# Later stores, gate temporaries in operand slots, one table load per output product, and an end in two halves, in a two-layer hybrid block on one core

## The chip, the core and the metric

The kernel runs on one core of a Trainium2 chip. The core has five engines with instruction queues of their own: TensorE (PE, matrix products), VectorE (DVE), ScalarE (ACT), GpSimd (POOL) and SyncE (SP, which here only issues transfers). Sixteen DMA engines move data between the device's memory and the core. ACT, SP and POOL can each issue transfers; in the profile they have the queues q10 (ACT), q1 (SP) and q0 (POOL). The metric is device time in microseconds (us) of one execution.

## The reference

One sequence of 512 tokens of width 2048 goes through two layers in float32. Both have the same frame:

```python
xn = rms_norm(h, norm_pre[i])
...                                  # the layer's mixing, ending in a product with w_out
h = h + rms_norm(y, norm_post[i])
h = h + (p[i] @ ple_w_proj[i]) * jax.nn.sigmoid(h @ ple_w_gate[i])
```

Layer 0 mixes with 16 heads of an attention with forgetting ("fox") and 16 heads of a recurrent time mix ("rwkv"), both gated by silu; layer 1 is a gated MLP with a spatial mix over chunks of 128 tokens:

```python
u, v, g = _split(xn @ c_w_in[j], (GMLP_W, GMLP_W, GMLP_W))        # 2048 columns each
v = layer_norm(gelu(v), c_ln_g, c_ln_b)
mixed = einsum('gts,bnsgc->bntgc', w_s * causal, v in chunks of 128 tokens and 16 groups) + b_s
y = (gelu(u) * mixed * silu(g)) @ c_w_out[j]
```

## The kernel before

**The order of the program.** Layer 0's input products and its rwkv part run first (to 730 us), then fox with the last gates (730 to 1011), the output product (1011 to 1180), the product with `ple_w_proj` (to 1202) and the gate product with `ple_w_gate` (to 1380). Layer 1's input product follows (1380 to 1853) in parts named V, U0, G0, U1 and G1, of which V is twice as long as the others, then its output product (to 2023), the small product (to 2045), the gate product (to 2207) and the last store. All float32 matmuls are made of three passes of a narrower type: each operand is split into a high and a low part, `whi`, `wlo` for weights, `xh`, `xl` for the other side, and hi*hi, hi*lo and lo*hi are summed.

**The Strassen products.** The large products use Strassen's scheme: seven products of half the size, numbered 1 to 7, in place of eight. `seven` runs over them, and in each over eight *pieces* of weights, two casts and 12 (or 24 half as wide) matmuls apiece. `pieces` yields them: a weight tile `rq`, `raw` or `half`, loaded by SP or POOL, is cast on ACT (L1559, `whi`) and its rest taken on DVE (L1561, `wlo`). The sums of activations that Strassen needs are made on DVE by `sums` (L1428, L1429), cast on ACT (L974) and taken again on DVE (L975).

**What sets the order.** A scheduler places the instructions of each engine by priority and by data dependencies; each engine then runs its own list in order. Two devices steer it. `later(n, step)` puts a piece of side work into the program n piece rows after the present one, and `tick` hands it out. `row()` (L977) ties an instruction to the latest weight cast, `self.cast`: it is not issued before that. Side work without such a tie can be placed much earlier than its row.

**The places the change touches.**

- *The mixed u.* In `layer_c`, `mix` norms one group of v (L1690), mixes it (L1720 to L1722, matmuls from `sg`, the cast of L1713), and multiplies u in place (L1724). Each mix takes its v from the device's memory (`sq<-vd`, L1673) and three small tables (L1680, L1684), all issued on ACT's queue. The mixed u, two tiles `u[0]` and `u[1]` of four rows, goes back to memory by `saved` (L1765 to L1767): eight stores `yd<-xh`, also on ACT's queue. U1's gelu (L1657) writes over them later.
- *The last gates.* In `layer_ab`, `load` and `gate` (L2020 to L2030) multiply the outputs of fox and rwkv by silu of 16 gate blocks. Gates 7, 0, 1, 2 are the last. Their inputs (`gz`, and `vT` for those copied from PSUM at L2049) and tanh results (`th`) lie in the pool `fw`, in fox's memory. The output product's weight tiles `rq` reuse that memory. `yh` slots are the places of later operands.
- *The table.* `row_scale` (L1218) makes 1/rms from sums of squares. It calls `row_rstd`, which takes a logarithm and an exponential on ACT. With `self.last` given, the load of their function table is issued after that instruction (`ln_exp`, ACT_TABLE_LOAD at L370).
- *The gate's sums.* `first_gate` puts sums for layer 1's first Strassen products into the rows of the gate product: `s1`, `s24`, `x22`, `s3`, four of each. `s24(q)` without a second argument forms the sum of `s1(q)` again.
- *The end.* `last_layer`'s `emit` (L1365) takes a block of 128 x 512: sigmoid on ACT, a multiplication and an addition on DVE, a store by SP. `seven` calls it for product 3 (L1614) after a subtraction on DVE (L1615).

Of the kernel before, what the change touches and what calls it, by code (L numbers as in the profile page):

```python
# [16 lines left out]
P = 128  # L17
T = 512
# [88 lines left out]
class Net:  # L107
# [991 lines left out]
    def first_gate(self, H, state, wp, ps):  # L1099
# [85 lines left out]
        W = i["ple_w_gate"][0]  # L1185
        self.seven(FIRST(*[Pair(W, 2 * j * T, 2 * j, emit) for j in range(2)]), Sets(s), ps, fm=True)
        s1, s24, s3, x22 = C[3:]
        steps = [(8 + 2 * q, lambda q=q: s1(q)) for q in range(4)]
        steps += [(17 + 4 * q, lambda q=q: s24(q)) for q in range(4)]
        steps += [(35 + 3 * q, lambda q=q: x22(q, True)) for q in range(4)]  # L1190
        steps += [(48 + 3 * q, lambda q=q: s3(q)) for q in range(4)]
        return accq, last["act"], cs, steps
# [1 line left out]
    def out_product(self, layer, W, swap, s, steps, place, load_place, hd, src_place, op_place, wp, ps):  # L1194


        nc, tc, i = self.nc, self.tc, self.i
        npost = self.cols["norm_post"]
        H, Y = {}, {}
        accq = [self.t(wp, [P, T], "accq", bufs=1), self.rstdB]  # L1200
        seen = [False, False]

        def out_block(pr, m, n, src):
            e, q = m // 2, 2 * n + m % 2
            Y[q, e] = place(q, e).rearrange("p (a t) -> p a t", a=2)
            sv = src.rearrange("p (a t) -> p a t", a=2)
            for a in range(2):
                c = 16 * layer + 2 * q + a
                self.last = nc.scalar.activation(Y[q, e][:, a, :], sv[:, a, :], AF.Copy, scale=npost[:, c : c + 1])
            if seen[e]:  # L1210
                sq = self.t(wp, [P, T], "sq")
                nc.scalar.activation(sq, src, AF.Square)
                nc.vector.tensor_tensor(accq[e], accq[e], sq, ALU.add)
            else:
                nc.scalar.activation(accq[e], src, AF.Square)
            seen[e] = True

        def row_scale(e):  # L1218
            with tc.high_priority(HP):
                pt = self.t(ps, [P, 256], "mm")  # L1220
                for a in range(2):
                    nc.tensor.matmul(pt, self.ones, accq[e][:, a * 256 : a * 256 + 256], start=(a == 0), stop=(a == 1))
                self.row_rstd(pt, accq[e][:, :256], self.last)

        def load(q):
            for e in range(2):
                H[q, e] = load_place(q, e).rearrange("p (a t) -> p a t", a=2)
                nc.sync.dma_start(H[q, e], hd[:, 2 * q : 2 * q + 2, e * 256 : e * 256 + 256])

        def ple():  # L1230
            self.pops = [], []
            for j in range(2):
                src = src_place(j).rearrange("p (m c) -> p m c", c=P)
                nc.sync.dma_start(src, i["p"][layer, 0, :, j * P : (j + 1) * P].rearrange("(m p) c -> p m c", p=P))
                pt = self.t(ps, [P, T], "mm")
                for m in range(4):
                    nc.tensor.transpose(pt[:, m * P : (m + 1) * P], src[:, m, :], self.ident)
                for ops, n in zip(self.pops, (2 * j, 2 * j + 1)):
                    ops.append(op_place(n))
                self.finish(pt, self.pops[0][j], self.pops[1][j])  # L1240

        steps = steps + [(88 + 3 * q, lambda q=q: load(q)) for q in range(8)]
        steps += [(82, ple), (98, lambda: row_scale(0))]
        for n, step in sorted(steps, key=lambda x: x[0]):
            self.later(n, step)
        pairs = [Pair(W, 2 * j * T, 2 * j, out_block) for j in range(2)]
        for pr in pairs:
            pr.swap = swap
        self.seven(FIRST(*pairs), Sets(s), ps, fm=True)
        self.clock += 100  # L1250
        self.tick()
        rows = lambda e: accq[e][:, :256].unsqueeze(1).broadcast_to([P, 2, 256])
        return H, Y, row_scale, rows

    def last_layer(self, cp, fs, turn, wp, ps):
# [106 lines left out]
        for n, step in sorted(steps, key=lambda x: x[0]):  # L1362
            self.later(n, step)

        def emit(pr, m, n, src):  # L1365
            nc.scalar.activation(src, src, AF.Sigmoid)
            nc.vector.tensor_tensor(src, src, pj[n, m], ALU.mult)
            o = res[n, m]
            nc.vector.tensor_tensor(o, o, src, ALU.add)
            self.later(  # L1370
                2, lambda: nc.sync.dma_start(self.out[0, m * P : (m + 1) * P, n * T : (n + 1) * T], o)
            )

        W = i["ple_w_gate"][1]
        pairs = [Pair(W, 2 * j * T, 2 * j, emit) for j in range(2)]
# [190 lines left out]
    def seven(self, order, sets, ps, after=lambda n: None, fm=False):  # L1566
# [3 lines left out]
        for step, (pr, prod, keep) in enumerate(order):  # L1570
# [30 lines left out]
            for m in range(2):  # L1601
                a = acc[m]
                if prod in (1, 5):
                    if m == 0:
                        pr.R[prod] = self.t(self.rp, [P, 2, T], "comb")
                    with tc.high_priority(2 * HP):
                        nc.scalar.copy(pr.R[prod][:, m], a)
                elif prod == 2:
                    pr.emit(pr, m, pr.n, a)
                elif prod == 6:  # L1610
                    u2 = pr.R[1][:, m]
                    nc.vector.tensor_tensor(u2, a, u2, ALU.add)
                elif prod == 3:
                    with tc.high_priority(HP) if step == len(order) - 1 else nullcontext():  # L1614
                        nc.vector.scalar_tensor_tensor(a, a, -1.0, pr.R[1][:, m], ALU.mult, ALU.subtract)  # L1615
                        pr.emit(pr, m, pr.n + 1, a)
            pr.done.add(prod)
            if prod == 7:
                u3 = pr.R[7] = pr.R[1] if 3 in pr.done else self.t(self.rp, [P, 2, T], "comb")
# [12 lines left out]
    def layer_c(self, cp, sets, steps, accq, after, wp, ps):  # L1632
# [129 lines left out]
            for e in range(2):  # L1762
                self.later(at + e, lambda e=e: turn(q, e, lambda a, m: y[a][:, m, :]))

        def saved(n):  # L1765
            for m in range(4):
                nc.scalar.dma_start(self.yd2[:, 4 * n : 4 * n + 4, m, :], u[n][:, m, :].rearrange("p (g c) -> p g c", c=P))  # L1767

        def done(step):
# [30 lines left out]
                    for e in range(8):  # L1800
                        mix(8 * j + e, 42 + int(6.8 * e))
            if step == nv + 13:
                for n in range(2):
                    self.later(4, lambda n=n: saved(n))
            if step == nv + 21:
                for q in range(4):
                    early(q, 26 + 5 * q)
# [178 lines left out]
    def layer_ab(self, cp, pool):  # L1986
# [26 lines left out]
        with tc.tile_pool(name="fc", bufs=1) as fc, tc.tile_pool(name="fw", bufs=2) as fw:  # L2013
# [3 lines left out]

            gz = {}

            def load(n):  # L2020
                gz[n] = self.t(fw, [P, T], "gz")
                nc.sync.dma_start(gz[n], self.ahead[C_GATES[n]])

            def gate(n):

                z, th = gz.pop(n), self.t(fw, [P, T], "th")
                with tc.issue_after(self.fox_ready.ins):
                    nc.scalar.activation(th, z, AF.Tanh, scale=0.5)
                nc.vector.scalar_tensor_tensor(self.y[n], z, 0.5, self.y[n], ALU.mult, ALU.mult)
                nc.vector.scalar_tensor_tensor(self.y[n], th, 1.0, self.y[n], ALU.add, ALU.mult)  # L2030

            self.Y11 = self.place(("yh", 8))
# [11 lines left out]
            load(7)  # L2044
            for n in range(3):
                acc = dense(C_GATES[n])
                gz[n] = self.t(fw, [P, T], "vT")
                with tc.high_priority(2 * HP):
                    copies = nc.scalar.copy(gz[n][:, :256], acc[:, :256]), nc.vector.tensor_copy(gz[n][:, 256:], acc[:, 256:])  # L2049
                    self.entry = [x.ins for x in copies]  # L2050
                gate(n)
# [31 lines left out]
```

## Time and profile before

Three runs took 2209.56, 2212.39 and 2212.74 us. The profile is of a further execution.

| | us |
|---|---|
| median of three runs | 2212.39 |
| the profiled execution | 2215.19 |
| its span, first to last instruction | 2213.5 |
| PE busy, 16535 matmuls | 2184.2 (99%) |
| DVE busy | 1663.0 (75%) |
| ACT busy | 1356.6 (61%) |
| POOL busy | 299.7 (14%) |
| DMA queues q1, q0, q10: share of 16 engines | 35.0%, 22.5%, 2.2% |
| last matmul starts | 2207.1 |

PE's 99% do not say that it runs without a break: matmuls are pipelined and their ends modelled, so that each shown duration (0.39 us for 512 columns) is longer than the distance to the next (0.23 us). What PE loses is therefore read from its idle times, from the clock that it was granted, and from the chain of work that ended last. In all rows a line number is that of the kernel before. The words after `<-` in brackets are what ended the idle time before an instruction.

### The profile page before, as it was taken

How to read it: one execution, taken by the hardware profiler on the slowest of the kernel's cores; microseconds unless marked ns; L12 is line 12 of the kernel's file. 1: busy time of each engine (PE TensorE's matmuls, PEld its weight loads, DVE VectorE, ACT ScalarE, POOL GpSimd, SP SyncE). 2: the span in 40 equal slices, each digit the busy share in tenths (PEclk: the TensorE clock that was granted, in tenths of full speed). 3: DMA queues.
4: the chain of work that ended last, by engine and by line, in shares of the span. 5: the costliest groups of instructions: out<-in, count | busy, mean ns of one | idle time of the engine just before them, and what ended most of it. 6: DMA issues, size and time to landing. Idle time of an engine off the chain costs nothing.

```text
span 2213.5 us, 43467 instructions
## 1 busy us (share of the span) xinstructions
PE 2184.2 (99%) x16535; PEld 1875.3 (85%) x16535; DVE 1663.0 (75%) x3228; ACT 1356.6 (61%) x2764; POOL 299.7 (14%) x360
## 2 busy tenths in 40 slices
PE   8999999999999999999999999999999999999998
PEld 7878888888888788888998999788887889999887
DVE  8756677657633678886978988997686688978978
ACT  5545555555544577775767757766575577757754
POOL 2001010101000000000220121111220221120031
PEclk9999999999999999999999999999999999999999
DMA  7322322223233733336797889788778787688796
GB/s 237 95 79 58 89 78 77 74 64 92 68 87 99 220 102 94 103 88 181 150 205 256 213 190 237 178 217 223 179 168 215 174 197 189 148 197 267 206 244 170
DMA packets 304143, 343.34 MB, mean 155 GB/s; under 512 B 15757, under 2 KB 187950, under 8 KB 302910
## 3 DMA queue, kind: packets, MB, share of 16 engines
q1 hardware_dynamic: 237438, 240.93, 35.0%
q0 software_dynamic: 44608, 85.99, 22.5%
q10 hardware_dynamic: 21888, 13.64, 2.2%
q8 instruction: 130, 2.13, 0.4%
q14 instruction: 79, 0.65, 0.1%
HBM read 305.61 MB, written 34.90 MB: 154 GB/s over the span
## 4 chain that ended last, share of the span: by engine, by line
PE 83%; DVE 6%; DMA 4%; issue 4%; ACT 3%; SPq 0%; ACTq 0%; POOL 0%; DVEq 0%; POOLq 0%
PE mm L1596 43%; PE mm L213 9%; PE mm L215 9%; PE mm L214 9%; DVE wlo L1561 2%; PE tm L551 1%; DMA rq<-in_ple_w_gate_dram 1%; PE tm L572 1%; PE g L923 1%; DMA sq<-vd 1%; PE tm L484 1%; PE tm L910 1%; PE pp L340 1%; ACT whi L197 1%; PE ch L636 1%
## 5 line engine op out<-in xcount | busy, mean ns | idle before, releaser
L1559 ACT CAST whi<-rq 128x512 fp32r<-128x512 f32 x485 | 299.0, 620 | 211.7 <-PE mm L1596 133.4
L1561 DVE TENSOR_TENSOR wlo<-rq,whi 128x512 fp32r<-128x512 f32 x485 | 331.6, 690 | 111.7 <-ACT whi L1559 109.6
L213 PE MATMUL mm<-xh,whi 128*128 128x512 f32 x992 | 412.1, 415 | 0.0
L215 PE MATMUL mm<-xh,wlo 128*128 128x512 f32 x992 | 391.8, 395 | 0.0
L214 PE MATMUL mm<-xl,whi 128*128 128x512 f32 x992 | 389.8, 393 | 0.0
L197 ACT CAST whi<-raw 128x512 fp32r<-128x512 f32 x272 | 167.5, 617 | 151.0 <-PE mm L214 106.3
L199 DVE TENSOR_TENSOR wlo<-raw,whi 128x512 fp32r<-128x512 f32 x272 | 186.1, 696 | 94.1 <-ACT whi L197 71.3
L215 PEld LDWEIGHTS mm<-xh,wlo 128*128 128x128 f32 x992 | 186.4, 188 | 41.3
L213 PEld LDWEIGHTS mm<-xh,whi 128*128 128x128 f32 x992 | 187.0, 189 | 33.2
L214 PEld LDWEIGHTS mm<-xl,whi 128*128 128x128 f32 x992 | 187.3, 189 | 29.8
L1596 PE MATMUL mm<-whi,xl 128*128 128x512 f32 x424 | 137.9, 392 | 0.8 <-DVE xl L975 0.4
L1596 PE MATMUL mm<-whi,yh 128*128 128x512 f32 x424 | 137.6, 393 | 0.0
L1596 PE MATMUL mm<-whi,yl 128*128 128x512 f32 x420 | 137.6, 393 | 0.0
L1561 DVE TENSOR_TENSOR wlo<-raw,whi 128x512 fp32r<-128x512 f32 x154 | 105.3, 690 | 40.1 <-ACT whi L1559 39.5
L1559 ACT CAST whi<-raw 128x512 fp32r<-128x512 f32 x154 | 94.9, 620 | 65.8 <-PE mm L1596 50.9
L1596 PE MATMUL mm<-xh,whi 128*128 128x256 f32 x696 | 126.9, 283 | 0.0
L1596 PEld LDWEIGHTS mm<-xh,whi 128*128 128x128 f32 x696 | 108.7, 192 | 0.1
L1504 POOL DMA_DIRECT2D rq<-in_c_w_in_dram x56 | 68.3, 1220 | 244.4 <-DVE wlo L1561 154.1
L1596 PE MATMUL mm<-xh,wlo 128*128 128x256 f32 x348 | 98.5, 283 | 0.0
L1561 DVE TENSOR_TENSOR half<-rq,half 128x512 fp32r<-128x512 f32 x111 | 76.5, 689 | 26.9 <-ACT half L1559 26.6
L1596 PE MATMUL mm<-xl,whi 128*128 128x256 f32 x520 | 95.5, 284 | 0.1
L1596 PEld LDWEIGHTS mm<-whi,xl 128*128 128x128 f32 x424 | 79.6, 188 | 18.2 <-DVE xl L975 0.9
(531 smaller groups left out, 5168.3 us busy)
## 6 DMA issues: line engine op xcount, KB each, us to landing
raw<-in_ab_w_in_dram SPq DMA_DIRECT2D x128, 512.0 KB, 3.9
rq<-in_c_w_in_dram POOLq DMA_DIRECT2D x56, 512.0 KB, 6.7
rq<-in_c_w_in_dram SPq DMA_DIRECT2D x50, 512.0 KB, 4.9
rq<-in_ple_w_gate_dram SPq DMA_DIRECT2D x44, 512.0 KB, 5.9
rq<-in_ple_w_gate_dram POOLq DMA_DIRECT2D x36, 512.0 KB, 9.1
raw<-in_c_w_in_dram SPq DMA_DIRECT2D x26, 512.0 KB, 7.8
rq<-in_c_w_out_dram SPq DMA_DIRECT2D x24, 512.0 KB, 4.4
rq<-in_ab_w_out_dram POOLq DMA_DIRECT2D x20, 512.0 KB, 7.4
```

What stands on the lines that cost most here:

```text
L197: nc.scalar.copy(hi[:, : m * n], src)
L199: self.weng.tensor_tensor(lo[:, : m * n], src, f(hi[:, : m * n]), ALU.subtract)
L213: nc.tensor.matmul(acc, hi, xhi[k], start=(k == 0), stop=False)
L214: nc.tensor.matmul(acc, hi, xlo[k], start=False, stop=False)
L215: nc.tensor.matmul(acc, lo, xhi[k], start=False, stop=(k == nk - 1))
L340: nc.tensor.matmul(acc, mat, part, start=(j == 0), stop=(j == 1))
L484: nc.tensor.matmul(pg[q][:, e], BK[pp, e].rearrange("p a t -> p (a t)"), AR[pp, e, q::2, :], start=True, stop=True)
L551: nc.tensor.matmul(px[dst, e, :], a[src, e, :], b[src, e, :], start=True, stop=True)
L1504: nc.gpsimd.dma_start(view(tl), block(*where), accum_op=ALU.add)
L1559: self.cast = nc.scalar.copy(hi, src)
L1561: nc.vector.tensor_tensor(lo, src, f(hi), ALU.subtract)
L1596: nc.tensor.matmul(o, x, y, start=(first and r == 0 and j == 0 and not a), stop=(r == 7 and j == 2), **more)
```

## The change

Five edits:

1. `saved` is called once for each of the eight stores, at rows 7 to 14 after U1's start instead of twice at row 4, and each store is tied by `row()` to the cast of its row.
2. For gates 7, 0, 1 and 2, `gz` lies in the `yh` slots 4, 5, 6 and 7, and tanh is written in place, except for gate 2, whose tanh goes to `yh` slot 3. For gates 7, 0 and 1 the first multiplication comes before tanh.
3. `row_scale` loads no table; one load is placed at row 66 of each output product.
4. In `first_gate`, `s24(q, s1(q))` at rows 8, 13, 18 and 23 takes the place of `s1` at rows 8 to 14 and `s24` at rows 17 to 29.
5. In the last product's second block, subtraction, sigmoid, multiplication, addition and store are each done for 256 columns and then for the other 256.

```diff
         s1, s24, s3, x22 = C[3:]
-        steps = [(8 + 2 * q, lambda q=q: s1(q)) for q in range(4)]
-        steps += [(17 + 4 * q, lambda q=q: s24(q)) for q in range(4)]
+        steps = [(8 + 5 * q, lambda q=q: s24(q, s1(q))) for q in range(4)]
...
-                self.row_rstd(pt, accq[e][:, :256], self.last)
+                self.row_rstd(pt, accq[e][:, :256], None)
...
+        def table():
+            with self.row():
+                nc.scalar.preload_act_table_set(LNSET)
+
-        steps = steps + [(88 + 3 * q, lambda q=q: load(q)) for q in range(8)]
+        steps = steps + [(88 + 3 * q, lambda q=q: load(q)) for q in range(8)] + [(66, table)]
...
-        def emit(pr, m, n, src):
-            nc.scalar.activation(src, src, AF.Sigmoid)
-            nc.vector.tensor_tensor(src, src, pj[n, m], ALU.mult)
+        def emit(pr, m, n, src, parts=(slice(0, T),), ready=lambda x: None):
+            for x in parts:
+                ready(x)
+                nc.scalar.activation(src[:, x], src[:, x], AF.Sigmoid)
             o = res[n, m]
-            nc.vector.tensor_tensor(o, o, src, ALU.add)
-            self.later(
-                2, lambda: nc.sync.dma_start(self.out[0, m * P : (m + 1) * P, n * T : (n + 1) * T], o)
-            )
+            for x in parts:
+                nc.vector.tensor_tensor(src[:, x], src[:, x], pj[n, m][:, x], ALU.mult)
+                nc.vector.tensor_tensor(o[:, x], o[:, x], src[:, x], ALU.add)
+                to = self.out[0, m * P : (m + 1) * P, n * T + x.start : n * T + x.stop]
+                self.later(2, lambda x=x, to=to: nc.sync.dma_start(to, o[:, x]))
...
+                    def less(x, a=a, m=m):
+                        nc.vector.scalar_tensor_tensor(a[:, x], a[:, x], -1.0, pr.R[1][:, m, x], ALU.mult, ALU.subtract)
+
                     with tc.high_priority(HP) if step == len(order) - 1 else nullcontext():
-                        nc.vector.scalar_tensor_tensor(a, a, -1.0, pr.R[1][:, m], ALU.mult, ALU.subtract)
-                        pr.emit(pr, m, pr.n + 1, a)
+                        if step == len(order) - 1 and m:
+                            pr.emit(pr, m, pr.n + 1, a, (slice(0, T // 2), slice(T // 2, T)), less)
+                        else:
+                            less(slice(0, T))
+                            pr.emit(pr, m, pr.n + 1, a)
...
-        def saved(n):
-            for m in range(4):
+        def saved(n, m):
+            with self.row():
                 nc.scalar.dma_start(self.yd2[:, 4 * n : 4 * n + 4, m, :], u[n][:, m, :].rearrange("p (g c) -> p g c", c=P))
...
             if step == nv + 13:
-                for n in range(2):
-                    self.later(4, lambda n=n: saved(n))
+                for x in range(8):
+                    self.later(7 + x, lambda x=x: saved(x // 4, x % 4))
...
+            own = {7: 4, 0: 5, 1: 6, 2: 7}
+
             def load(n):
-                gz[n] = self.t(fw, [P, T], "gz")
+                gz[n] = self.slot("yh", own[n], F32) if n in own else self.t(fw, [P, T], "gz")
                 nc.sync.dma_start(gz[n], self.ahead[C_GATES[n]])
...
-                z, th = gz.pop(n), self.t(fw, [P, T], "th")
+                z = th = gz.pop(n)
+                if n == 2:
+                    th = self.slot("yh", 3, F32)
+                elif n not in own:
+                    th = self.t(fw, [P, T], "th")
+                if n in own and n != 2:
+                    nc.vector.scalar_tensor_tensor(self.y[n], z, 0.5, self.y[n], ALU.mult, ALU.mult)
                 with tc.issue_after(self.fox_ready.ins):
                     nc.scalar.activation(th, z, AF.Tanh, scale=0.5)
-                nc.vector.scalar_tensor_tensor(self.y[n], z, 0.5, self.y[n], ALU.mult, ALU.mult)
+                if n not in own or n == 2:
+                    nc.vector.scalar_tensor_tensor(self.y[n], z, 0.5, self.y[n], ALU.mult, ALU.mult)
...
-                gz[n] = self.t(fw, [P, T], "vT")
+                gz[n] = self.slot("yh", own[n], F32)
```

The order of instructions changes at three places of which the prediction speaks. In the order rows the lines are those of the kernel named; L1500 and L1559 of the kernel before are L1505 and L1564 of the changed one.

The first is ACT's list in G0's last rows, where the stores of the mixed u stand in the kernel before (L1767, `yd` from `xh`), among weight casts, a mix's tables (`accq`) and v (`sq`). Before:

```order
L1690 ACTIVATE sq_20053<-sq_20053,nb_17484,rv_17483 128x128 x3
L1767 DMA yd_36_104<-xh_3789_19158 128x4x128
L1559 CAST whi_20198<-rq_3993_20084 128x512
L1712 CAST w_4019_20208<-mm_20134 128x128
L1767 DMA yd_36_104<-xh_3789_19158 128x4x128
L1559 CAST whi_20218<-rq_3993_20084 128x512
L1680 DMA accq_20196<-in_c_ln_g_dram 128x128
```

The changed kernel, in U1's first product, up to its gelu (the table load of L1668 is L1657's before):

```order
L1778 DMA yd_36_104<-xh_3782_19146 128x4x128
L1778 DMA yd_36_104<-xh_3840_19415 128x4x128
L1564 CAST whi_20611<-rq_4098_20598 128x512
L1564 CAST whi_20624<-rq_4103_20622 128x512
L1778 DMA yd_36_104<-xh_3840_19415 128x4x128
L1564 CAST whi_20634<-rq_4103_20622 128x512
L1778 DMA yd_36_104<-xh_3840_19415 128x4x128
L1564 CAST half_4111_20650<-rq_4067_20457 128x512
L1778 DMA yd_36_104<-xh_3840_19415 128x4x128
L1564 CAST whi_20660<-rq_4067_20457 128x512
L1564 CAST whi_20671<-rq_4072_20479 128x512
L1564 CAST whi_20681<-rq_4072_20479 128x512
```

`xh_3782` is u[0], of which the fourth store is shown, and `xh_3840` is u[1]. No store stands in G0 any more; all eight stand between the casts of U1's first pieces, and the gelu's table load follows the last row.

The second is SP's list at the entry of the first output product, with the weight loads. Before:

```order
L1500 DMA raw_12752<-in_ab_w_out_dram 128x2x512
L1500 DMA raw_12792<-in_ab_w_out_dram 128x2x512
L1500 DMA raw_13070<-in_ab_w_out_dram 128x2x512
L1500 DMA raw_13104<-in_ab_w_out_dram 128x2x512
L1500 DMA rq_2602_12866<-in_ab_w_out_dram 128x2x512
L1500 DMA rq_2612_12911<-in_ab_w_out_dram 128x2x512
```

And in the changed kernel:

```order
L1505 DMA raw_12749<-in_ab_w_out_dram 128x2x512
L1505 DMA raw_12789<-in_ab_w_out_dram 128x2x512
L1505 DMA rq_2599_12863<-in_ab_w_out_dram 128x2x512
L1505 DMA rq_2609_12908<-in_ab_w_out_dram 128x2x512
L1505 DMA rq_2616_12948<-in_ab_w_out_dram 128x2x512
L1505 DMA rq_2621_12982<-in_ab_w_out_dram 128x2x512
L1505 DMA rq_2629_13023<-in_ab_w_out_dram 128x2x512
L1505 DMA raw_13067<-in_ab_w_out_dram 128x2x512
```

Five `rq` loads now stand ahead of two `raw` loads that they followed.

The third is ACT's list at the entry of the first gate product: scales and squares of the output blocks (L1209 and L1212 before, L1208 and L1211 changed), a weight cast, the table load, and the copies out of PSUM (L1093). Before:

```order
L1093 COPY yl_2976_15041<-mm_14991 128x512
L1209 ACTIVATE yh_2956_14968<-comb_14347,col_72_254 128x256
L197 CAST whi_15132<-raw_15114 128x512
L1209 ACTIVATE yh_2956_14968<-comb_14347,col_72_254 128x256
L1212 ACTIVATE sq_14971<-comb_14347 128x512
L1212 ACTIVATE sq_14978<-comb_12906 128x512
L1209 ACTIVATE yh_2960_14982<-comb_12906,col_72_254 128x256 x2
L197 CAST whi_15182<-raw_15180 128x512
L370 ACT_TABLE_LOAD
L1212 ACTIVATE sq_14985<-comb_12906 128x512
L1093 COPY yl_2977_15044<-mm_14992 128x512
```

And in the changed kernel:

```order
L1211 ACTIVATE sq_14975<-comb_12903 128x512
L1208 ACTIVATE yh_2957_14979<-comb_12903,col_72_254 128x256
L197 CAST whi_15178<-raw_15176 128x512
L1208 ACTIVATE yh_2957_14979<-comb_12903,col_72_254 128x256
L1211 ACTIVATE sq_14982<-comb_12903 128x512
L1093 COPY yl_2972_15035<-mm_14987 128x512
L1093 COPY yl_2973_15038<-mm_14988 128x512
L1093 COPY yl_2974_15041<-mm_14989 128x512
```

The table load is gone from here, and the first two copies, which stood ahead of the last squares, now come behind them.

## The prediction

> **What bounds the kernel now.** I read the page's chain first, then TensorE's (PE's) waits, then windows around the largest of them.
>
> ```profile
> PE 83%; DVE 6%; DMA 4%; issue 4%; ACT 3%; SPq 0%; ACTq 0%; POOL 0%; DVEq 0%; POOLq 0%
> ```
>
> PE is 83% of the chain that ends last, and the change takes away no matmul. So it can only win where PE stands still or runs slowly. PE's waits that lie near the edits (in all, times, longest):
>
> ```profile
> PE mm L1720 <- ACT sg L1713: 5.3, 1, 5.3
> PE mm L1596 <- ACT whi L1559: 2.4, 1, 2.4
> ...
> PE mm L999 <- ACT yl L1093: 0.9, 1, 0.9
> ...
> PE mm L1222 <- ACT yl L1093: 0.5, 1, 0.5
> PE mm L1596 <- DVE xl L975: 0.4, 1, 0.4
> PE mm L1596 <- ACT xl L974: 0.4, 1, 0.4
> ```
>
> Behind three of them stands a second loss, seen in windows (stretch, length, busy time of PE, PEld, DVE, ACT and POOL, then the clock granted to PE, DMA share, GB/s):
>
> ```profile
> 1025.00:1028.40 3.40, 3.40 (x18) 3.40 (x18) 3.20 (x7) 2.20 (x5) 1.43 (x2) 0.51 0.93 348
> 1195.60:1199.00 3.40, 3.30 (x8) 2.65 (x9) 0.40 (x2) 2.27 (x6) 0.00 (x0) 0.50 0.87 242
> 1675.20:1680.30 5.10, 5.10 (x12) 3.69 (x13) 3.89 (x6) 2.05 (x5) 0.00 (x0) 0.50 0.37 106
> ```
>
> Just after each stall PE's clock is 0.50 or 0.51. At half speed a stretch costs half its length: 1.7 us at 1025, 1.7 at 1195.6, 2.6 at 1675. The three places lose 2.4 + 1.7 = 4.1, 0.9 + 0.5 + 1.7 = 3.1 and 5.3 + 2.6 = 7.9 us: 15.1 in all. The change touches the cause of each.
>
> The Trainium skill ("TensorE: Matmul & The Clock Gate", Part 1: The HAM clock gate) says that the clock falls after at least one idle window of about 3.4 us. The rows differ: it fell after 2.4 us, and after 0.9 + 0.5. By the rule only the 7.9 us would go entirely and the two 1.7 us might stay, a gain lower by 3.4 us; I go by the rows.
>
> **Stores of the mixed u.** Why did PE wait 5.3 us? ACT's timeline has it:
>
> ```profile
> 1650.61 0.38 ACTq L1767 DMA_DIRECT2D yd<-xh  x1
> ...
> 1652.78 0.38 ACTq L1767 DMA_DIRECT2D yd<-xh  x1
> ...
> 1658.77 1.00 ACTq L1673 DMA_DIRECT2D sq<-vd  x1
> ...
> 1673.74 0.88 ACT L1690 ACTIVATE sq<-sq,nb,rv 128x128 f32<-128x128 f32 x2 [5.85 <-DMA sq<-vd]
> ```
>
> Two of the eight stores went out early and stand in ACT's DMA queue, q10, ahead of the next mix's three tables and of its v (sq<-vd). V arrived some 15 us after its issue. ACT stood 5.85 us on it, with the cast L1713 that PE wanted queued behind. What q10 moved (packets, MB, share) from 1650.6 to 1658.8, with the issues of a store and of a table in that stretch, and from 1658.8 to 1673.7:
>
> ```profile
> q10 hardware_dynamic: 762, 0.53, 27.8%
> ...
> yd<-xh ACTq DMA_DIRECT2D x2, 256.0 KB
> ...
> accq<-in_c_ln_g_dram ACTq DMA_DIRECT2D x1, 64.0 KB, 17.2
> ```
>
> ```profile
> q10 hardware_dynamic: 1080, 0.70, 16.3%
> ```
>
> It ran at 0.53/8.2 = 65 KB/us, then at 0.70/14.9 = 47. The sum, 1.23 MB, is two stores of 256 KB (0.52), three tables of 64 KB (0.20), this v (0.26 as a store), and 0.25 left over from before. Without the stores 0.71 MB remain, and by 1658.8 the left-over and the tables can be through (0.45 of the 0.53 moved by then). V's own 0.26 MB take 4.0 us at 65 and 5.6 at 47: it lands near 1663 to 1665, with 2 us on the way by 1667. ACT began its idle at 1673.74 less 5.85, at 1667.9. So v comes in time, or 0 to 0.8 us late. I take 7.9 us, the whole; bounds 4 and 8.3: under 4, v would land after 1670, at half the slower rate; the upper end adds the 0.4 that the store issues take ACT's queue.
>
> The stores move to rows 7 to 14 of U1's first product, eight within some 11 us. What is late next is U1's gelu, which overwrites the old u:
>
> ```profile
> 1714.84 1.28 ACT L1657 ACT_TABLE_LOAD   x1 [0.65 <-DMA yd<-xh]
> ```
>
> Today it waits 0.65 us, with four stores ahead of it in q10 from 1697.5 on. After the change four must land too, u[0]'s, since u[1]'s come behind; so about the same wait. A second wait is new: by the built program, the last two stores wait on ACT, ahead of its casts, for a landed u[0] store and for a weight load of this kind:
>
> ```profile
> 1701.70 3.74 SPq L1500 DMA_DIRECT2D raw<-in_c_w_in_dram  x2
> ```
>
> ```profile
> raw<-in_c_w_in_dram SPq DMA_DIRECT2D x2, 512.0 KB, 8.0
> ```
>
> Issued at 1701.7, it lands 8.0 us later, at 1709.7; the last store's place in ACT's order is that of the cast at 1709.5. More traffic may add some us: ACT waits 0 to 3. PE has casts in hand, as these rows show:
>
> ```profile
> 1665.91 0.63 ACT L1559 CAST half<-rq 128x512 fp32r<-128x512 f32 x1 [0.75 <-PE mm L1596]
> ```
>
> ```profile
> 1679.69 1.83 PE L1596 MATMUL mm<-half,yh 128*128 128x512 f32 x6
> ```
>
> Cast at 1665.9, read at 1679.7, less some 7.4 us lost in between: 6 us ahead, of which 2 are the cast and DVE's pass. Up to 4 us of ACT's wait is hidden: cost 0; beyond it PE pays one for one.
>
> **The entry of the output product.**
>
> ```profile
> 1002.70 0.58 ACT L928 COPY yl<-g 64x512 f32<-64x512 f32 x1 [0.53 <-PE g L923]
> ```
>
> ```profile
> 1014.83 0.70 DVE yl L2030
> 1015.62 6.79 DMA rq<-in_ab_w_out_dram
> ```
>
> ```profile
> 1022.48 1.14 ACT L1559 CAST whi<-rq 128x512 fp32r<-128x512 f32 x2 [3.09 <-DMA rq<-in_ab_w_out_dram]
> ```
>
> The first rq load lies in fox's memory, where the last gates' temporaries are alive until DVE's L2030 ends at 1015.5. In the change they lie in operand slots, and rq waits only for fox, whose last product is copied at 1002.70. SP then issues five rq loads from about 1003 to 1007, and at 6.8 us they land near 1010 to 1014, where the cast would take the first at 1019.4 (1022.48 less 3.09). The 2.4 us and the half clock behind them go: 4.1. The gates' instructions keep kind and number; where tanh is now in place it waits for DVE's first multiply, 0.69 us under PE's matmuls. But ACT and DVE are full here with the gates' casts, so up to 1 us of another wait may show, and with it the clock. I take 4; bounds 1 and 5.
>
> **Table loads.** In the entry of the gate product PE waits for ACT's copies out of PSUM:
>
> ```profile
> 1191.24 1.28 ACT L370 ACT_TABLE_LOAD   x1
> 1192.53 0.63 ACT L1212 ACTIVATE sq<-comb 128x512 f32<-128x512 f32 x1
> 1193.07 0.57 ACT L1093 COPY yl<-mm 128x512 f32<-128x512 f32 x1
> ```
>
> ```profile
> 1193.69 0.50 PE L999 MATMUL mm<-xl,whi 128*128 128x512 f32 x1 [0.94 <-ACT yl L1093]
> ```
>
> The load leaves: 1.28 us of ACT's queue ahead of those copies. But the new order also puts every block's scale and square ahead of the first copy, where two copies stood between them. Counting its rows by these durations, the first copy ends near 1192, and PE wants it about 0.9 us earlier: of 1.4 us of waits 0.9 remain, and the half clock perhaps not. I take 2 of the 3.1; bounds -0.5 (clock still down, the copy later yet) and 3.1. The one load that is left, at row 66, runs between casts for which ACT has time. The second layer has no such wait: 0.
>
> **The gate's sums.** Four sums leave DVE:
>
> ```profile
> L1428 DVE TENSOR_TENSOR sg<-yl,yl x16: 420/422/432, 1015.8 to 1080.2; 128x256 f32<-128x256 f32 x16
> L1428 DVE TENSOR_TENSOR sg<-yh,yh x16: 684/688/697, 1205.4 to 1432.2; 128x512 f32<-128x512 f32 x16
> ```
>
> That is 4 x 0.69 = 2.8 us of DVE work up to 1432, just ahead of layer C's first products, where PE waits 0.4 + 0.4 for xl. Earlier sums take both; other waits may take their place. 1 us, bounds -0.5 and 1.5.
>
> **The end in halves.** DVE, the serial tail, does six passes over 256 columns for three over 512. By the two rows above that is 6 x 0.42 - 3 x 0.69 = 0.45 more, less the overlap with ACT's sigmoid, and less half of the last store of 256 KB. 0, bounds -0.4 and 0.4.
>
> **The sum** is 7.9 + 4 + 2 + 1 + 0 = 14.9 us, from the profiled execution's 2215.2 to 2200.3. That execution lies 2.8 above the runs' median, 2212.4; part of that may be the stalls themselves. I take 13.4 from the median: **2199.0**.
>
> **The rivals.** *A: v still comes late.* q10 shares the DMA engines with POOL's and SP's loads, so v may land near 1670 without the stores too. PE then waits some 2.5 us plus a halved clock of 1.7: of the 7.9, 3.7 remain: 2199.0 + 4.2 = 2203, up to 2207. For it: v's margin of 1 us. Against it: the 0.52 MB counted above.
>
> *B, the slower side: the burst of stores holds ACT.* If the eight stores do not land in their order, u[0]'s last comes with the whole burst. 2.1 MB at the mean of 65 and 47 KB/us take 37 us, to 1734 on the old clock, where U1's gelu wants it at 1714.8. ACT's casts stand behind it; with 4 us hidden PE waits some 15 and runs 2.6 us of half clock: 2199.0 + 17.6 = 2217, and from 2211 if half of it. It decides from 4 us of ACT's idle at this table load. For it: nothing but the larger burst. Against it: today's 0.65 us behind four stores. The Trainium skill ("DMA: Bandwidth & Descriptors", Queues, rings and completion order) says that each engine takes a ring's descriptors in ring order, which speaks against it; no row here shows two stores of one queue apart.
>
> *C: the instructions move and the time does not.* Each stall removed uncovers the next one: four waits of other operands lie within 1 us behind the entry's, and weight loads, 3 to 8 us earlier for PE, are just in time. 2207 to 2212.
>
> **How the numbers follow.** Forecast (2193.5 to 2203) 0.58, A 0.18, B 0.10, C 0.14. No change means within 0.2%, 4.4 us, about what a measurement of this kernel can tell. Below 2208.0 lie the forecast, A and a third of C: faster 0.80. The rest of C and half of B are the same: 0.14. Slower 0.06. The range: 2193.5 is all terms at their upper bounds (8.3 + 5 + 3.1 + 1.5 + 0.4 = 18.3) off the median; 2208.5 takes in A and part of C and leaves under 0.2 out.
>
> **What would show it.** The wait of L1720 on L1713 is gone from PE's list, and no half clock stands where 1675 was; likewise at 1025 and 1195. The first rq load is issued near 1003. Two table loads are gone, and the one of row 66 has no wait of PE behind it. Wrong would be: ACT still idle for sq<-vd by over 2 us; ACT idle for over 4 us at a store or at U1's gelu; a PE wait on whi in U1.

## The result, and the profile after

The changed kernel takes 2200.21 us (median of five runs, 2198.46 to 2202.32) against 2212.39 (five runs): a ratio of 0.9949, 95% interval 0.9934 to 0.9963, or 11.3 us less (8.2 to 14.6). The forecast was 2199.0. A second series, beside other experiments, gave 0.9943 (0.9930 to 0.9955).

The profiled execution has a span of 2200.6 us, 12.9 less than the one before. Its list of PE's waits, cut where layer 0's small ones stand:

```profile
PE mm L1601 <- DVE yh L2069: 0.9, 1, 0.9
PE mm L1601 <- ACT whi L1564: 0.9, 1, 0.9
...
PE mm L1601 <- DVE wlo L1566: 0.7, 2, 0.4
PE mm L1601 <- DVE xh L975: 0.6, 1, 0.6
```

Line L1596 of the kernel before is now L1601. The wait of 5.3 us for `sg`, that of 2.4 for `whi` at the entry, those for `yl` and those for `xl` are gone from it. The windows over four places (columns as in the prediction) have a full clock. They are the entries of the output product and of the gate product, V's end, and the place of L1720's wait:

```profile
1005.00:1028.00 23.00, 22.08 (x158) 20.55 (x157) 18.56 (x37) 14.12 (x26) 2.96 (x3) 1.00 0.79 228
1176.00:1199.00 23.00, 23.00 (x106) 19.15 (x105) 21.18 (x36) 21.12 (x44) 0.00 (x0) 1.00 0.65 223
1497.00:1510.00 13.00, 11.79 (x51) 9.18 (x51) 7.57 (x14) 5.97 (x11) 0.00 (x0) 1.00 0.88 247
1655.00:1675.00 20.00, 19.76 (x86) 15.77 (x86) 16.42 (x28) 12.93 (x27) 0.43 (x1) 1.00 0.87 249
```

The third is new: PE lost 1.2 us at V's end, where before it lost nothing.

PE issues the same matmuls in nearly the same order in all kernels here, so stages can be compared exactly: the time from one matmul to another, by their numbers in PE's list, in one trace less that in another. This table is worked out so. Each entry is the difference from the first profile of the kernel before, in us; the columns are this kernel, two experiments told below and a second profile of the kernel before.

| stage (matmuls) | changed | stores alone | end alone | before, again |
|---|---|---|---|---|
| layer 0 up to fox (0 to 8160) | +1.4 | -0.4 | -1.2 | -0.8 |
| entry of the output product (9360 to 9480) | -4.6 | 0.0 | 0.0 | -2.2 |
| entry of the gate product (10700 to 11000) | -3.9 | -3.6 | -3.6 | -3.6 |
| V's first products (12400 to 12760) | -1.3 | 0.0 | -0.1 | 0.0 |
| V's end (12760 to 12900) | +1.7 | +4.0 | 0.0 | +0.2 |
| G0's end (13400 to 13620) | -7.3 | -8.0 | -0.7 | -0.8 |

The first row has the same instructions in all four and still differs by up to 2.5 us. The third row is the surprise: it is as large where the code there was not touched.

### The profile page after: what moved, and what is told of

Same layout as the page of the kernel before. It is cut to its first block, busy times and chain, and to the rows that moved or that the text cites. A ratio compares the mean times of both kernels' runs of the same rounds, so it can differ in the third digit from the quotient of the medians.

```text
span 2200.6 us, 43486 instructions
## 1 busy us (share of the span) xinstructions
PE 2176.7 (99%) x16535; PEld 1870.7 (85%) x16535; DVE 1661.6 (76%) x3227; ACT 1354.0 (62%) x2763; POOL 298.4 (14%) x360
## 4 chain that ended last, share of the span: by engine, by line
PE 89%; DMA 4%; DVE 3%; ACT 2%; issue 1%; SPq 0%; ACTq 0%; DVEq 0%; POOLq 0%
PE mm L1601 46%; PE mm L213 10%; PE mm L215 9%; PE mm L214 9%; DMA rq<-in_ple_w_gate_dram 2%; PE tm L551 1%; PE tm L572 1%; DMA gz<-gd 1%; PE g L923 1%; DVE wlo L1566 1%; PE pp L340 1%; PE tm L484 1%; PE ch L636 1%; PE tm L910 1%; PE ch L637 1%
## 5 line engine op out<-in xcount | busy, mean ns | idle before, releaser
L1564 ACT CAST whi<-rq 128x512 fp32r<-128x512 f32 x485 | 298.7, 621 | 203.4 <-PE mm L1601 126.1
L1601 PE MATMUL mm<-whi,yh 128*128 128x512 f32 x424 | 137.0, 391 | 0.9 <-ACT whi L1564 0.9
L1601 PE MATMUL mm<-whi,xl 128*128 128x512 f32 x424 | 137.7, 392 | 0.0
L1601 PE MATMUL mm<-whi,yl 128*128 128x512 f32 x420 | 137.6, 393 | 0.0
L1564 ACT CAST whi<-raw 128x512 fp32r<-128x512 f32 x154 | 94.7, 620 | 60.8 <-PE mm L1601 46.6
L1601 PE MATMUL mm<-xh,whi 128*128 128x256 f32 x696 | 126.9, 283 | 0.0
L1601 PEld LDWEIGHTS mm<-xh,whi 128*128 128x128 f32 x696 | 108.7, 192 | 0.1
L1601 PE MATMUL mm<-xh,wlo 128*128 128x256 f32 x348 | 98.5, 283 | 0.0
L1564 ACT CAST half<-rq 128x512 fp32r<-128x512 f32 x111 | 68.9, 620 | 47.6 <-PE mm L1601 27.6
L1601 PE MATMUL mm<-xl,whi 128*128 128x256 f32 x520 | 95.5, 284 | 0.1
```

Of the source, the lines that this page charges most:

```text
L1564: self.cast = nc.scalar.copy(hi, src)
L1601: nc.tensor.matmul(o, x, y, start=(first and r == 0 and j == 0 and not a), stop=(r == 7 and j == 2), **more)
```

## The experiments

### Each edit alone

Five kernels, each the kernel before with one of the five edits.

```diff
+            with self.row():                                  # stores alone; the eight calls at rows 7 to 14
                 nc.scalar.dma_start(self.yd2[...], u[n][:, m, :]...)
...
+                gz[n] = self.slot("yh", own[n], F32)          # entry alone; load, gate and copies as in the change
...
+        ... + [(66, table)]                                   # table alone; row_rstd(..., None)
...
+        steps = [(8 + 5 * q, lambda q=q: s24(q, s1(q))) for q in range(4)]   # sums alone
...
+            pr.emit(pr, m, pr.n + 1, a, (slice(0, T // 2), slice(T // 2, T)), less)   # end alone
```

> The kernel before with the tied stores alone. Theory (ring order: the two early stores delay v): the wait of PE's L1720 falls from 5.3 us to under 1, the half clock behind it goes, and the time is 7 to 8 us lower. Rival (v is late because all DMA engines are full): PE still waits 2 us or more for that cast, 3 to 4 us lower. Rival (burst holds ACT): PE waits over 2 us in U1, and the time is the same or higher.

> The kernel before with the gates' temporaries in operand slots alone. Theory: PE's wait of 2.4 us at the output product's entry and the half clock of 3.4 us behind it go: 4 us lower. By the skill's clock rule (one idle window of 3.4 us) the half clock would have another cause and might stay: 2.4 us lower. Rival (the next wait takes the place): 0 to 1 us lower.

> The kernel before with the table loads moved alone. Prediction: 2 us lower, with a wait of 0.9 us for a copy out of PSUM left. The changed kernel's trace shows no wait left there, so theory now: 3 to 4 us lower, the waits of 0.9 and 0.5 us and the half clock all gone. Rival (the gain there came from the order of the sums or the earlier entry, not from the loads): less than 1 us.

> The kernel before with the merged sums of the gate product alone. Theory: PE's waits for xl of 0.4 and 0.4 us and some before them go, 1.4 to 1.7 us up to layer 1's second Strassen product; but PE then reaches the end of V earlier, where ACT waits for a weight load, and gives all of it back near 1510: 0 in all, within 0.7 us. Rival: the late weight load has nothing to do with it, and 1.5 us stay.

> The kernel before with the end in halves alone. The trace of the change shows 1.3 us more between the last matmul's start and the end than before (7.7 for 6.4): theory, the halves run one after the other since each waits for the whole tile's last writer, so the time is 1.3 us higher, give or take 0.3. Prediction: 0, within 0.4.

| kernel | ratio to before, 95% interval | us |
|---|---|---|
| stores alone | 0.9972 (0.9963 to 0.9981) | -6.2 (-8.2 to -4.2) |
| entry alone | 0.9986 (0.9978 to 0.9995) | -3.1 (-4.9 to -1.1) |
| table alone | 0.9993 (0.9984 to 1.0002) | -1.5 (-3.5 to +0.4) |
| sums alone | 1.0003 (0.9994 to 1.0012) | +0.7 (-1.3 to +2.7) |
| end alone | 1.0002 (0.9994 to 1.0011) | +0.4 (-1.3 to +2.4) |

They add up to -9.7 us, near the whole change's -11.3. Two edits carry it; the other three can't be told from nothing by the runs.

*Stores.* The wait of L1720 is gone from PE's list, and ACT waits 0.3 us for v:

```profile
ACT sq L1690 <- DMA sq<-vd: 0.3, 1, 0.3
```

*Entry.* The stage is 4.6 us shorter. The window from 1006 to 1030, in the kernel before and with the entry alone:

```profile
1006.00:1030.00 24.00, 20.43 (x134) 18.86 (x133) 15.15 (x30) 11.59 (x22) 2.55 (x2) 0.93 0.63 201
```

```profile
1006.00:1030.00 24.00, 23.08 (x166) 21.59 (x165) 19.11 (x37) 14.37 (x27) 3.75 (x3) 1.00 0.76 224
```

In the same 24 us PE begins 166 matmuls in place of 134, and the half clock goes with the stall. The rule that the prediction weighed (the Trainium skill, "TensorE: Matmul & The Clock Gate", Part 1: The HAM clock gate: at least one idle window of about 3.4 us) gives no reason for a half clock behind a stall of 2.4 us.

*Table.* The entry of the gate product is 3.9 us shorter, as the newer theory in the expectation has it. But it is also 3.6 us shorter in the kernels with the stores alone, the entry alone and the end alone (3.2 with the sums alone), which do not touch it. The next experiment asks why.

*Sums.* PE's two waits for `xl` are gone and V's first products are 0.8 us shorter; V's end is 2.5 us longer. That fits the theory in the expectation, but V's end is taken up again below.

*End.* The tail of the span, from the start of the last matmul to the last event, is 7.7 us here and in both profiles of the changed kernel, and 6.4 without the edit. So the end costs 1.3 us in every trace. The runs' interval holds both that and nothing.

### The kernel before, profiled again

No edit.

> The kernel before, profiled a second time. In the first profile ACT waited 3.2 us for a weight load of the small product and PE lost 3.1 us in the gate product's entry; nine profiles of other kernels show 0 to 1.5 us for that load and no such loss. Theory (that loss belongs to one execution, not to the kernel): PE waits under 0.5 us for copies there and no half clock. Rival (the kernel before always has it): 0.9 and 0.5 us again, with a half clock. The losses at the output product's entry (2.4 us) and at L1720 (4 us or more) come again in both.

The loss in the gate product's entry did not come again; the other two did. The window from 1176 to 1202, first profile and second:

```profile
1176.00:1202.00 26.00, 24.51 (x117) 20.06 (x116) 21.12 (x35) 21.17 (x42) 0.00 (x0) 0.93 0.60 207
```

```profile
1176.00:1202.00 26.00, 25.97 (x128) 21.71 (x127) 23.95 (x40) 25.33 (x50) 0.00 (x0) 1.00 0.68 235
```

What differed is seen on ACT, at its first cast of the small product's weights, again first and second:

```profile
1177.04 0.62 ACT L197 CAST whi<-raw 128x512 fp32r<-128x512 f32 x1 [3.16 <-DMA raw<-in_ple_w_proj_dram]
```

```profile
1171.79 0.62 ACT L197 CAST whi<-raw 128x512 fp32r<-128x512 f32 x1 [0.90 <-PE mm L1596]
```

In the first profile ACT waited 3.2 us for a weight load. Full from there on, it never caught up, and its copies for PE were late some 15 us further on. In all other profiles of this study ACT's wait for that load was 0 to 1.5 us, and PE waited 0.4 us or less for those copies. The load was issued late: at 1168.82, 7.0 us before PE's matmul 10700, and in the second profile at 1163.99, 8.8 us before it. SP first had eight loads of operands to issue, which took it longer, first profile and second:

```profile
1156.55 10.31 SPq L1228 DMA_DIRECT2D xh<-xd  x8
```

```profile
1153.57 8.47 SPq L1228 DMA_DIRECT2D xh<-xd  x8
```

The table load that stands just ahead of the copies does not make PE wait by itself: it is there in six other profiles too, and their stage is 3.2 to 3.6 us shorter. Whether taking it out would help in an execution with a late weight load is not shown. That the late weight load is the cause is read from the traces; it was not reproduced on purpose.

PE's waits of this second profile at the two other places:

```profile
PE mm L1720 <- ACT sg L1713: 4.1, 1, 4.1
...
PE mm L1596 <- ACT whi L1559: 1.7, 1, 1.7
```

They are the kernel's own, though smaller than in the first profile, and the entry's 1.7 us was not followed by a half clock. In the four other profiles with early stores on ACT's queue, L1720's wait is 3.8 to 6.2 us.

### Stores early, but in another queue

Is v late because it stands behind the stores, or because all DMA engines are full? Here the stores go out as early as before, but through POOL's queue.

```diff
-                nc.scalar.dma_start(self.yd2[:, 4 * n : 4 * n + 4, m, :], ...)
+                nc.gpsimd.dma_start(self.yd2[:, 4 * n : 4 * n + 4, m, :], ...)
```

> The kernel before with the eight stores issued by POOL: two still go out early, but in POOL's queue and not ahead of v. Theory (v stands behind the stores in ACT's queue): ACT waits under 1.5 us for sq<-vd near 1670 and PE's L1720 under 1 us; a price may show at a weight load, which POOL issues behind the stores. Rival (the DMA engines are full, whatever the queue): ACT waits 3 us or more for sq<-vd.

The ratio is 0.9967 (0.9955 to 0.9979), -7.3 us: the whole gain of the tied stores. Two stores were issued at 1639.7, and v was 0.8 us late:

```profile
1639.72 1.57 POOL L1767 DMA_DIRECT2D yd<-xh  x2 [1.21 <-DVE xh L1724]
```

```profile
1665.62 0.50 ACT L1690 ACTIVATE sq<-sq,nb,rv 128x128 f32<-128x128 f32 x1 [0.81 <-DMA sq<-vd]
```

V was issued at 1654.1, so it took 11.4 us, as in the changed kernel (11.0), for 14.9 before. The DMA engines were just as full while it was under way (DMA share next to last; this kernel first, then the kernel before):

```profile
1650.00:1658.00 8.00, 8.00 (x37) 6.59 (x36) 5.72 (x11) 5.16 (x12) 3.31 (x3) 1.00 1.12 208
1658.00:1665.00 7.00, 7.00 (x32) 5.77 (x31) 6.91 (x13) 4.61 (x10) 0.28 (x1) 1.00 1.07 250
```

```profile
1650.00:1658.00 8.00, 8.00 (x37) 6.57 (x36) 6.98 (x12) 5.46 (x11) 4.40 (x5) 1.00 1.05 200
1658.00:1665.00 7.00, 7.00 (x33) 5.71 (x32) 5.41 (x10) 5.59 (x12) 0.00 (x0) 1.00 1.11 232
```

So full engines alone do not make v late, and that rival falls. The kernel itself does not part one thing: POOL issued the stores 11 us earlier than ACT had, and they landed by 1650.9. They were out of v's queue and also out of its time.

The packets of the traces part it. On q10 stores and tables go in pieces of 512 B and v in 128 pieces of 2 KB, so one can count what moved between v's issue and its landing. These are q10's packets, MB and share in that time in the changed kernel and in this one (the kernel before had 1080 packets and 0.70 MB, as the prediction shows):

```profile
q10 hardware_dynamic: 576, 0.46, 15.5%
```

```profile
q10 hardware_dynamic: 576, 0.46, 14.2%
```

In each of the eight profiles without early stores on ACT's queue, 384 small pieces, which are the three tables, moved after v's issue. In the six with them it was 609 to 865. The pieces moved no slower there (44 to 70 in a us, for 41 to 52), but there were more of them, and v's last piece ended 12.8 to 15.0 us after v's issue, for 9.6 to 11.3. So v waits for what stands ahead of it in its queue. That also explains the 11 us that are left: in the changed kernel the tables' pieces take until 7.6 us after v's issue, and v's own take 3.9 us, most of them behind the tables.

### Stores five rows later

```diff
-                    self.later(7 + x, lambda x=x: saved(x // 4, x % 4))
+                    self.later(12 + x, lambda x=x: saved(x // 4, x % 4))
```

> The changed kernel with the tied stores five rows later (rows 12 to 19), so that u[0]'s last is issued some 5 us nearer to U1's gelu. It tests from when the burst would cost: theory, ACT's wait at the gelu's table load grows to 4 to 8 us and PE, which has 4 us in hand, waits 0 to 4 us in U1, with a halved clock if over 2: the time 0 to 6 us above the changed kernel. If PE does not wait with ACT over 4 us idle, the slack was put too small.

The ratio is 0.9950 (0.9936 to 0.9963), the changed kernel's. ACT did not wait for a landing at U1's gelu:

```profile
1695.29 0.37 ACTq L1778 DMA_DIRECT2D yd<-xh  x1
...
1702.09 0.62 ACT L1564 CAST whi<-rq 128x512 fp32r<-128x512 f32 x1 [0.74 <-DVE wlo L1566]
1702.73 1.28 ACT L1668 ACT_TABLE_LOAD   x1
```

u[0]'s fourth store is the one of 1695.29, the first was issued at 1690.60. All four had landed by 1702.7: 1.05 MB in at most 12.1 us, 87 KB/us or more, where the prediction went by 47 to 65. The wait of 4 to 8 us that the expectation forecast for ACT did not come up. So this says nothing on how long a wait of ACT is hidden from PE, only that five rows of room were left.

### The changed kernel without the end, without the sums, and again

```diff
-        steps = [(8 + 5 * q, lambda q=q: s24(q, s1(q))) for q in range(4)]      # without the sums
+        steps = [(8 + 2 * q, lambda q=q: s1(q)) for q in range(4)]
+        steps += [(17 + 4 * q, lambda q=q: s24(q)) for q in range(4)]
...
-                            pr.emit(pr, m, pr.n + 1, a, (slice(0, T // 2), slice(T // 2, T)), less)   # without the end
+                            pr.emit(pr, m, pr.n + 1, a)
```

> The changed kernel, beside the others of this call: 12 us lower than before.

> The changed kernel with the end as it was. By the theory on the end 1.3 us lower than the changed kernel; by the prediction the same within 0.4.

> The changed kernel with the gate's sums as they were. Theory (V's end is bound by a weight load, which gives an earlier PE its lead back): PE's wait near 1506 shrinks by about what the sums lose, and the time is that of the changed kernel within 0.7 us. Rival: 1 to 1.7 us higher.

| kernel | ratio to before, 95% interval | median us |
|---|---|---|
| the changed kernel again | 0.9943 (0.9930 to 0.9955) | 2197.84 |
| without the end | 0.9943 (0.9930 to 0.9955) | 2199.72 |
| without the sums | 0.9949 (0.9936 to 0.9963) | 2200.29 |

*Without the end* the runs are the same. The trace's tail is 6.4 us again, from 7.7. Why the halves cost is seen in DVE's and ACT's rows of the changed kernel, after the last matmul's start at 2192.90:

```profile
2193.33 0.43 DVE L1620 SCALAR_TENSOR_TENSOR mm<-mm,comb 128x256 f32<-128x256 f32 x1
2193.67 0.68 DVE L1375 TENSOR_TENSOR xh<-xh,mm 128x512 f32<-128x512 f32 x1
2193.80 0.37 ACT L1371 ACTIVATE mm<-mm 128x256 f32<-128x256 f32 x1 [1.19 <-DVE mm L1620]
2194.26 0.43 DVE L1620 SCALAR_TENSOR_TENSOR mm<-mm,comb 128x256 f32<-128x256 f32 x1
...
2194.72 0.37 ACT L1371 ACTIVATE mm<-mm 128x256 f32<-128x256 f32 x1 [0.56 <-DVE mm L1620]
2195.12 0.43 DVE L1374 TENSOR_TENSOR mm<-mm,xh 128x256 f32<-128x256 f32 x1 [0.43 <-ACT mm L1371]
2195.59 0.42 DVE L1375 TENSOR_TENSOR xh<-xh,mm 128x256 f32<-128x256 f32 x1
2196.05 0.43 DVE L1374 TENSOR_TENSOR mm<-mm,xh 128x256 f32<-128x256 f32 x1
2196.51 0.42 DVE L1375 TENSOR_TENSOR xh<-xh,mm 128x256 f32<-128x256 f32 x1
```

The same in the kernel before, after the last matmul's start at 2207.10:

```profile
2207.53 0.70 DVE L1615 SCALAR_TENSOR_TENSOR mm<-mm,comb 128x512 f32<-128x512 f32 x1
2208.13 0.68 DVE L1369 TENSOR_TENSOR xh<-xh,mm 128x512 f32<-128x512 f32 x1
2208.26 0.58 ACT L1366 ACTIVATE mm<-mm 128x512 f32<-128x512 f32 x1 [1.46 <-DVE mm L1615]
...
2208.87 0.70 DVE L1367 TENSOR_TENSOR mm<-mm,xh 128x512 f32<-128x512 f32 x1
2209.61 0.69 DVE L1369 TENSOR_TENSOR xh<-xh,mm 128x512 f32<-128x512 f32 x1
```

There the sigmoid was already hidden: DVE meanwhile did an addition of the block before (2208.13). In halves, the second subtraction begins only after the first half's sigmoid, and the first half's multiplication only after the second half's sigmoid. Both instructions carry a wait for ACT in the trace: the two halves of one tile are ordered as if they were the same data. The first of these waits costs nothing, since DVE has that addition to do (2193.67); the second is the 0.43 us of idle time at 2195.12. With some 0.4 us for the greater number of passes, DVE ends 4.0 us after the last matmul's start, for 3.2 in the kernel before. Behind DVE the smaller last store is done 0.4 us sooner after its issue, but the program's closing waits on SP run 0.9 us longer. These figures are the same, within 0.05 us, in all profiles with the edit, and likewise in all without it.

*Without the sums* PE did not wait near 1506, and V's end was 0.3 us longer than in the first profile before, for 1.5 and 1.7 in the two of the changed kernel. V's first products were 0.7 to 1.3 us longer. Together that is the same time, as the theory in the expectation has it. But V's end varies as much by itself: up to there the kernel with the stores alone has the same instructions as the kernel before, and its V's end took 4.0 us more. These are ACT's waits for the weight load there in all profiles, without the merged sums: 2.7, 2.8, 3.0, 3.0, 3.2, 3.9, 4.8, 5.2; with them: 4.0, 4.2, 4.3, 4.5, 5.0, 5.3. PE paid from between 3.0 and 3.9 us on. The earlier PE probably adds to the wait, but the two sets overlap, and it is not shown.

### The last stores of v later

This is an attempt on that weight load. Two of V's stores of v, which run beside it, are tied behind it. They are not the last: in the trace four more follow some 17 us later.

```diff
+            def store():
+                with self.row():
+                    nc.scalar.dma_start(self.vd[...], dst...)
+            if n == 3 and m < 2:
+                self.later(8 + 2 * m, store)
+            else:
+                nc.scalar.dma_start(self.vd[...], dst...)
```

> The changed kernel with V's last two stores of v tied some rows later, behind the weight load that ACT waits for near 1500 (4.2 to 4.5 us, of which PE pays 1.2 to 1.7). Theory: 0.39 MB less in the DMA queues there, so ACT waits about 1 us less, and the time is 0.5 to 1 us lower. Rival (the load is late by its issue, or by POOL's accumulating loads alone): the same.

The ratio is 0.9945 (0.9931 to 0.9958), the changed kernel's; ACT waits 4.0 us, for 4.2 and 4.5. A change of 0.2 to 0.5 us in the wait can't be told from its spread, so neither theory is settled. No version here beats the changed kernel by what can be measured.

## Why the prediction was right

The time was predicted within 1.2 us, and the two large terms, stores and entry, came about by the mechanism that was forecast. Not every term of the sum held: one was an accident of the profile, and small ones of both signs stood beside it. So the closeness of the number is in part luck. In the changed kernel's trace, against the first profile and with 0.3 for the table in place of the accident, the stages give 7.3 (stores) + 4.6 (entry) + 0.3 (table) + 1.3 - 1.7 (sums, with V's end) - 1.3 (end) = 10.5 us. The runs say 11.3 (8.2 to 14.6).

- **Stores, 7.9 predicted.** The mechanism holds: the queue's order, shown by two kernels that take the stores out of v's way, one later, one through another queue, and by the count of the pieces. Measured 6.2 (4.2 to 8.2) alone, 7.0 to 8.1 in the stage against the first profile, 6.2 to 7.3 against the second, whose own wait was smaller. V's landing was forecast as in time or up to 0.8 us late; ACT waited 0.97 us. The way was longer, though: v was issued at 1651.5 and landed near 1662.5, 11 us later, where the prediction had 4 to 8. The step that was off is that the tables can be through when v is issued. All their 384 pieces were still to come and took 7.6 us, 26 KB/us where the prediction had 47 to 65. That the wait still came out as forecast is in part luck: ACT reached it 10.1 us after v's issue, for 9.1 in the kernel before, and PE has no wait from what remained.
- **The new wait of the last store, 0 to 3 us on ACT, hidden.** It is there and hidden: the issue took 2.00 us, ACT stood 1.48 us before its next cast, where 0.7 is usual there, and PE has no wait near it.

```profile
1695.91 2.00 ACTq L1778 DMA_DIRECT2D yd<-xh  x1
1698.00 1.25 ACT L1564 CAST whi<-rq 128x512 fp32r<-128x512 f32 x2 [1.48 <-DVE half L1566]
```

- **Entry, 4 predicted.** Five rq loads were issued from 1003.66, and no cast waited for them:

```profile
1003.66 2.75 SPq L1505 DMA_DIRECT2D rq<-in_ab_w_out_dram  x5
```

The stage is 4.6 us shorter against the first profile, 4.2 to 5.0 against all six without this edit in which the clock fell there, and 2.45 against the second profile, which had no half clock. The runs say 3.1 (1.1 to 4.9). The feared new wait did not come.
- **Table loads, 2 predicted.** The step that failed is its first sentence, that in this entry PE waits for ACT's copies: it did so in one execution. In its place the runs showed 0.3 us for the stage where the weight load is in time (3.9 less 3.6), and 1.5 (-0.4 to 3.5) in the time. The forecast of a wait of 0.9 us that remains was wrong too: none did. The row that told it, ACT's 3.16 us for a load at 1177, stands in the trace 14 us ahead of the first row that the prediction shows of this stage.
- **Sums, 1 predicted.** The waits for `xl` went, 0.7 to 1.4 us; V's end was longer by as much or more in all six profiles with the edit. The size was wrong by about 1 us, within the stated bounds. That the sums cause the loss at V's end is not shown.
- **End, 0 predicted.** The step that failed is the overlap with ACT's sigmoid: it was there before, and in halves 0.43 us of it is lost. The tail is 1.3 us longer, outside the bounds of 0.4. The 0.4 us that a smaller last store saves were rightly counted; the 0.9 us of longer closing waits were not in the sum.
- **The median.** 13.4 was taken from the median in place of the sum's 14.9, since the profiled execution lay 2.8 us above it. That went the right way. The reason given, that a part may be the stalls themselves, fits the table's stage, whose 3.6 us belong to that execution; but the first 767 us vary by as much, so this is not shown. The lower end of the range is off by a slip: 2212.4 less 18.3 is 2194.1, not 2193.5. Nothing hangs on it.

Rival A fell with the stores in POOL's queue. Rival B fell in the changed kernel itself, where ACT had no wait at U1's table load, and again with the stores five rows later. C can hold at V's end alone, for 1.5 to 1.7 us in the changed kernel, and even there the same loss came without any edit ahead of it.

## What to carry to other kernels

A transfer that nobody needs soon can be costly by its place: here two stores of 256 KB delayed the small load behind them on the same queue, and the engine that waited for that load delayed a third. Count what stands ahead of the load in pieces too, not in bytes alone: 0.2 MB of tables in pieces of 512 B took twice as long as 0.26 MB of v in pieces of 2 KB. Tie such a store to where the queue is idle, or move it to another queue. Before a stall in a profile is put down to the instruction next to it, follow the engine that is late back to its own last wait, and profile the kernel twice: what does not come again is not there to be gained. Splitting a tile's work into halves gains no overlap if the two halves' dependencies are kept by the tile.

## What was not expected of the hardware

The clock's fall is not set by the length of a stall alone. In all 14 profiles PE stood still for 0.5 and then 0.6 us near 163 us. Behind that the clock halved for 3.4 us in six of them, among these one of the two profiles of the changed kernel, and not in the other eight. At V's end it halved after waits of 1.4 and 0.3 us in the kernel with late stores, and not after 1.7 and 0.3 us in that with the sums alone. At the entry of the output product it halved after 2.0 to 2.7 us in six profiles and not after 1.7 us in the seventh, which length alone would explain. How long it stays halved is not set by the stall alone either: at L1720's wait it was 3.4 us in a profile with a wait of 5.0, and 6.8 us in one with 4.1.

And with the same instructions the first 767 us of the program took up to 4 us more in one execution than in another (from -1.8 to +2.2 against the first profile). The half clock near 163 us is in part of them and, by an estimate from its 3.4 us at half speed, accounts for 1.7 us. This is why a change of 1 us can be read in a stage of the trace and not in the time.
